# The first layer's memory stage: values for two k tiles ahead of the keys, key weights in 2 KB rows, and the finished values cast ahead of the next group's weights

## The chip, the core and the metric

The kernel runs on one core of one Trainium2 chip. The metric is the device time of one execution in microseconds (us). Three timed runs of the kernel before the change gave 897.07, 897.88 and 898.92 us; the median, 897.88 us, is the number that the change is measured against.

The engines are named as in the profile: PE multiplies matrices (PEld is its weight load, which overlaps), DVE and ACT are the two vector engines that do the casts and subtractions here, POOL issues the small transfers of turned tiles, and SP issues the loads of inputs and weights. All arithmetic on PE is on 32-bit numbers in the format `float32r`.

## The reference, cut to what matters

Two layers; each is one mixer with three head groups (banded chunk attention, gated linear attention, cross-attention into 256 memory tokens), a gate path, an output projection and a layer norm. The change touches only the projection of the memory tokens in the first layer, whose results are the keys and values of the cross-attention:

```python
mkv = mem @ w_mem_kv                    # (256, 2048) @ (2048, 1024)
mk, mv = jnp.split(mkv, 2, axis=-1)     # keys and values, 512 columns each
heads_m = lambda t: t.reshape(t.shape[0], t.shape[1], M_HEADS, M_HEAD_DIM)
y_m = memory_attention(heads_m(m_q), heads_m(mk), heads_m(mv)).reshape(B, S, M_WIDTH)
```

## The kernel before, in words

**Products.** A product in full 32-bit precision is made of three products of split operands: each operand is split into a rounded part `hi` (a cast) and a rest `lo = src - hi`, and `hi*hi + lo*hi + hi*lo` is summed in PSUM. `parts` does one split: the cast on ACT (L128), then the subtraction on DVE (L129). So every weight tile passes from a `raw` tile (the landing place of its DMA) into a `wh` and a `wl` tile, and every activation quarter into the two halves of an `x` tile. `as_products` issues the three matmuls of 128x512 for one k tile (128 of the 2048 inner elements) and one half `t` of the 256 tokens. There are four buffers each of `raw`, `wh` and `wl`.

**The memory stage (`first_memory`).** It comes first in the program. Two accumulators of two banks each are open: `accv` for the values and `acck` for the keys, the only two buffers of their kind. Eight pieces `p` follow each other, each with two k tiles `kk`; `first_pieces` loads and splits one piece: the memory tokens (`memT`, which lands in the space of `res`), the values' weights (a `raw` tile) and the keys' weights (another). The keys' weights lie in DRAM as two column halves of 256 each, and one row of 1024 numbers per partition holds two pieces; a piece's half is 2 k tiles x 256 numbers in a row there.

- For `p` of 0 and 1 the order is written out by hand on every engine: for each k tile the tokens, the values' weights, the keys' weights; PE takes values then keys of k tile 0, then values and keys of k tile 1. In the first k tile the values are cut into two halves of 256 columns, one of them loaded by ACT's queue.
- For `p` from 2 the loads and splits are for whole pieces of 128x1024, and PE takes both k tiles of the values, then both of the keys.
- The keys of piece 6 are kept back (`late`) until after the values of piece 7: the values are then complete, `parts(*mv, accv)` copies them from PSUM into the tiles `mv` (cast on ACT, subtraction on DVE), and PE has the keys of pieces 6 and 7 to go on with meanwhile.

The next group on PE is `as_group(halves(G_BQK), ...)`. It needs an accumulator of the same kind, and so the buffer of `accv`, which is free when both instructions of `mv` have read it. `each(p)` loads and splits a quarter of the layer's input `xT` after pieces 2, 4, 6 and 7 (`resident_quarter`, DMA on L164).

**What sets the order.** PE, SP and POOL work in program order. On ACT and DVE a scheduler that simulates times places the instructions, by priority: what stands under `tc.high_priority(AHEAD)` (the loads and splits of weights and input) goes ahead of what does not (the split into `mv` here). `placed_here` (`tc.keep_in_program_order`) holds an instruction in its place among the others so held. A DMA on SP waits until the buffer it writes is free, and some wait for the landing of an earlier DMA that used the same semaphore; everything behind it on SP waits with it.

Of the kernel before, what the change touches and what calls it, by code (L numbers as in the profile page):

```python
# [36 lines left out]
def hybrid_trunk_kernel(  # L37
# [88 lines left out]
    def parts(hi, lo, src, keep=lambda ins: ins):  # L126

        keep(act.copy(hi, src))  # L128
        keep(dve.tensor_tensor(lo, src, hi.bitcast(F32), op=ALU.subtract))  # L129
# [10 lines left out]
    def piece(src, n, kp=2, home=None):  # L140

        with tc.high_priority(AHEAD):
            raw = wp.tile([P, kp, n], F32, name=nm("raw"), tag="raw")
            if home is None:
                hi, lo = (wp.tile([P, kp, n], F32R, name=nm(w), tag=w) for w in ("wh", "wl"))
            else:
                hi, lo = home
            if isinstance(src, list):
                at = 0
                for part in src:  # L150
                    if len(part.shape) == 2:
                        part = part.rearrange("p (k n) -> p k n", k=kp)
                    sp.dma_start(raw[:, :, at:at + part.shape[2]], part)
                    at += part.shape[2]
            else:
                sp.dma_start(raw.rearrange("p k n -> p (k n)"), src)
            parts(hi, lo, raw)
# [10 lines left out]
    def first_pieces(p, x):  # L168
# [5 lines left out]
        ksrc = w512[0, G_MK, p // 2:8:4, :, j0 * 256:j0 * 256 + 512].rearrange("h p (k n) -> p k h n", k=2)  # L174
        raws, his, los = ([wp.tile([P, 2, 512], dt, name=nm(n), tag=n) for _ in range(2)]
                          for n, dt in (("raw", F32), ("wh", F32R), ("wl", F32R)))

# [8 lines left out]
        def split(i, at):  # L186
            parts(his[i][at], los[i][at], raws[i][at])

        if p < 2:
            with tc.manual_schedule(engines={DVE, mybir.EngineType.Activation}):  # L190
# [6 lines left out]
                for k in range(2):  # L197
                    x_part(slice(j0 + k, j0 + k + 1))
                    for i, at in enumerate(cuts[k]):
                        if i or len(cuts[k]) == 1:  # L200
                            sp.dma_start(raws[0][at], vsrc[at])  # L201
                        split(0, at)
                    sp.dma_start(raws[1][:, k].rearrange("p (h n) -> p h n", h=2), ksrc[:, k])
                    split(1, (slice(None), k))
        else:
            with tc.high_priority(AHEAD):
                x_part(slice(j0, j0 + 2))
                sp.dma_start(raws[0], vsrc)
                split(0, slice(None))
                for h in range(2):  # L210
                    sp.dma_start(raws[1][:, :, h * 256:(h + 1) * 256], ksrc[:, :, h])
                split(1, slice(None))
        return list(zip(his, los))

    def first_memory(mv, each):
# [22 lines left out]
        for p in range(8):  # L238
# [3 lines left out]
            for kk in range(2):  # L242
                values_of(p, v, kk)
                if p < 2:
# [3 lines left out]
            elif p > 1:  # L248
                if p == 7:
                    parts(*mv, accv)  # L250
# [4 lines left out]
            each(p)  # L255
# [10 lines left out]
    def as_group(src, xq, n, kp=2, first=None, need={}):  # L266

        acc = psd.tile([P, 2, 512], F32, name=nm("acc"), tag="acc")
        for pc in range(16 // kp):
# [3 lines left out]
            w = piece(src[pc], n, kp)  # L273
# [563 lines left out]
    for l in range(L):  # L837
# [47 lines left out]
        acc = as_group(halves(G_BQK), xq, 512)  # L885
# [274 lines left out]
```

## Time and profile before

| | |
|---|---|
| timed runs, us | 897.07, 897.88 (median), 898.92 |
| span of the profiled execution, us | 896.4 |
| instructions | 13888 |
| PE busy, us and share of the span | 887.2, 99% |
| DVE busy | 617.4, 69% |
| ACT busy | 482.1, 54% |
| mean granted clock of PE | 0.997 |
| moved by DMA | 216.90 MB, mean 242 GB/s |

The profiled execution has its span on record, from the first to the last instruction, and no timed number of its own; the median of the timed runs is 1.5 us over that span. Times inside the execution are us from the start of the span. In the timeline a row gives start, duration, engine, line, output<-inputs and shape, how many instructions were merged, and in brackets the engine's idle time before and what ended it. The row of a DMA issue (SPq, ACTq) gives the time that issuing took; the view of DMAs gives the time from issue to landing.

### The profile page before, as it was taken

How to read it: one execution, taken by the hardware profiler on the slowest of the kernel's cores; microseconds unless marked ns; L12 is line 12 of the kernel's file. 1: busy time of each engine (PE TensorE's matmuls, PEld its weight loads, DVE VectorE, ACT ScalarE, POOL GpSimd, SP SyncE). 2: the span in 40 equal slices, each digit the busy share in tenths (PEclk: the TensorE clock that was granted, in tenths of full speed). 3: DMA queues.
4: the chain of work that ended last, by engine and by line, in shares of the span. 5: the costliest groups of instructions: out<-in, count | busy, mean ns of one | idle time of the engine just before them, and what ended most of it. 6: DMA issues, size and time to landing. Idle time of an engine off the chain costs nothing.

```text
span 896.4 us, 13888 instructions
## 1 busy us (share of the span) xinstructions
PE 887.2 (99%) x4669; PEld 743.5 (83%) x4669; DVE 617.4 (69%) x905; ACT 482.1 (54%) x698; POOL 231.0 (26%) x431
## 2 busy tenths in 40 slices
PE   9999999999999999999999999999999999999996
PEld 7878988888988888888888888888888888888885
DVE  6756568767467676665595786896664758676866
ACT  6644475555446575543465545754754557565440
POOL 0022103114305353410034230231061444432300
PEclk9999999999999999999999999999999999999998
DMA  9988779867979797975689968696589897979752
GB/s 310 312 241 245 215 245 265 275 197 225 275 253 241 236 274 236 307 241 193 224 267 268 265 195 282 201 287 210 154 234 293 242 260 236 276 222 281 223 179 95
DMA packets 166088, 216.90 MB, mean 242 GB/s; under 512 B 25232, under 2 KB 143376, under 8 KB 166016
## 3 DMA queue, kind: packets, MB, share of 16 engines
q1 hardware_dynamic: 148256, 173.29, 63.7%
q0 software_dynamic: 17472, 42.33, 16.4%
q8 instruction: 37, 0.61, 0.3%
q10 hardware_dynamic: 288, 0.39, 0.1%
q14 instruction: 35, 0.29, 0.1%
HBM read 194.78 MB, written 21.10 MB: 241 GB/s over the span
## 4 chain that ended last, share of the span: by engine, by line
PE 98%; DVE 1%; DMA 0%; ACT 0%; issue 0%; SPq 0%; DVEq 0%
PE acc L102 91%; PE bk L102 6%; DMA raw<-w 0%; ACT wh L128 0%; DVE mv L129 0%; ACT res L823 0%; DVE wl L129 0%; PE bk L665 0%; DVE stats L809 0%; DVE res L808 0%; SPq L201 0%; DVE res L759 0%; SPq L179 0%; DVE mvt L762 0%; PE bk L812 0%
## 5 line engine op out<-in xcount | busy, mean ns | idle before, releaser
L102 PE MATMUL acc<-wh,x 128*128 128x512 f32 (+2 forms) x2516 | 747.8, 381 | 1.3 <-DVE mv L129 0.7
L102 PEld LDWEIGHTS acc<-wh,x 128*128 128x128 f32 x2516 | 460.6, 188 | 88.2 <-PE acc L102 1.1
L129 DVE TENSOR_TENSOR wl<-raw,wh 128x1024 fp32r<-128x1024 f32 (+3 forms) x321 | 368.4, 1152 | 198.9 <-ACT wh L128 187.0
L128 ACT CAST wh<-raw 128x1024 fp32r<-128x1024 f32 (+3 forms) x321 | 318.5, 996 | 344.2 <-PE acc L102 201.7
L102 PE MATMUL acc<-wl,x 128*128 128x512 f32 (+2 forms) x1258 | 475.9, 379 | 0.0
L102 PEld LDWEIGHTS acc<-wl,x 128*128 128x128 f32 x1258 | 236.0, 188 | 45.3 <-DVE wl L129 0.4
L527 POOL DMA_DIRECT2D home<-sc x76 | 42.5, 560 | 426.2 <-DVE sc L525 417.6
L532 POOL DMA_DIRECT2D pT<-home x96 | 52.4, 552 | 30.2 <-DMA home<-sc 12.1
L532 POOL DMA_DIRECT2D qk<-home x64 | 34.9, 553 | 36.5 <-DMA home<-sc 26.2
L532 POOL DMA_DIRECT2D zT<-home x48 | 26.2, 551 | 20.5 <-DMA home<-sc 14.0
L525 DVE STREAM_TRANSPOSE sc<-sc 128x512 f32<-128x512 f32 (+1 forms) x38 | 24.9, 668 | 3.7 <-ACT sc L996 3.0
L532 POOL DMA_DIRECT2D yr<-home x48 | 26.3, 557 | 3.2 <-DMA home<-sc 3.2
L525 DVE STREAM_TRANSPOSE sc<-acc 128x512 f32<-128x512 f32 x28 | 18.3, 691 | 4.3 <-PE acc L102 4.3
L554 ACT ACTIVATE sc<-sc,mx 128x128 f32<-128x128 f32 (+1 forms) x32 | 14.3, 448 | 8.9 <-DVE mx L552 8.8
L547 DVE SCALAR_TENSOR_TENSOR sc<-bk,bias 128x384 f32<-128x384 f32 x16 | 8.6, 539 | 10.7 <-PE bk L102 10.7
L128 ACT CAST x<-sc 128x512 fp32r<-128x512 f32 x20 | 12.2, 617 | 5.2 <-DVE sc L508 3.2
L532 POOL DMA_DIRECT2D xT<-home x24 | 13.2, 552 | 6.9 <-DMA xT<-home 5.2
L129 DVE TENSOR_TENSOR x<-sc,x 128x512 fp32r<-128x512 f32 x20 | 13.5, 685 | 1.4 <-ACT x L128 1.4
L102 PE MATMUL bk<-qk,qk 128*128 128x128 f32 (+1 forms) x64 | 13.1, 326 | 0.0
L698 DVE SCALAR_TENSOR_TENSOR res<-res,acc 128x512 f32<-128x512 f32 x15 | 9.7, 682 | 4.7 <-PE acc L102 4.7
L532 POOL DMA_DIRECT2D yT<-home x16 | 8.8, 555 | 14.8 <-DMA home<-sc 14.8
L129 DVE TENSOR_TENSOR x<-res,x 128x512 fp32r<-128x512 f32 (+2 forms) x13 | 10.0, 790 | 2.0 <-ACT x L128 2.0
(210 smaller groups left out, 524.3 us busy)
## 6 DMA issues: line engine op xcount, KB each, us to landing
raw<-w SPq DMA_DIRECT2D x387, 256.0 KB, 4.6
raw<-w SPq DMA_DIRECT2D x62, 512.0 KB, 5.0
home<-sc POOLq DMA_DIRECT2D x60, 256.0 KB, 4.4
raw<-w SPq DMA_DIRECT2D x32, 388.0 KB, 5.1
raw<-w SPq DMA_DIRECT2D x32, 264.0 KB, 3.5
qk<-home POOLq DMA_DIRECT2D x64, 64.0 KB, 4.7
raw<-w SPq DMA_DIRECT2D x32, 124.0 KB, 4.8
bias<-relw SPq DMA_DIRECT2D x16, 192.0 KB, 4.4
```

The source lines that it names most:

```text
L102: pe.matmul(o, l, r, start=start, stop=stop, skip_group_check=True)
L128: keep(act.copy(hi, src))
L129: keep(dve.tensor_tensor(lo, src, hi.bitcast(F32), op=ALU.subtract))
L525: dve.transpose(blocks.rearrange(order, j=32), src.rearrange("p (g b j) -> p g b j", b=4, j=32))
L527: pool.dma_start(homes[-1], blocks)
L532: pool.dma_start(dst[b * 32:(b + 1) * 32], home[:, b].rearrange("(a i) n -> i a n", a=4))
L547: dve.scalar_tensor_tensor(s, pb[:, :384], SCALE, bias[h], op0=ALU.mult, op1=ALU.add)
L554: act.activation(s[:, own[t]], s[:, own[t]], AF.Exp, bias=mx[:, t:t + 1], accum_out=zs[:, t:t + 1])
L698: dve.scalar_tensor_tensor(r, r, ALPHA, acc, op0=ALU.mult, op1=ALU.add)
```

## The change

- In `first_pieces` for `p` of 0 and 1, tokens and values' weights of both k tiles are loaded and split first, then the keys' weights. PE follows: values of both k tiles, then keys of both.
- The keys' weights of a piece are loaded as they lie: two DMAs, one per column half, each a row of 512 numbers (2 KB) per partition, for every `p`. Before, a DMA read rows of 256 numbers (1 KB): for `p` of 0 and 1 one DMA per k tile with both halves, from piece 2 on one per half. The tile now holds half, k tile, column in that order, and the split reads it through a view that puts the k tile first; `wh` and `wl` are laid out as before. The split of a k tile of the keys now needs both DMAs.
- `each(7)`, the last input quarter, moves ahead of `parts(*mv, accv)`, and the two instructions of `mv` are held in program order. The cast of the first weight piece of `G_BQK` in the first layer is held in program order behind them.

```diff
-    def parts(hi, lo, src, keep=lambda ins: ins):
-        keep(act.copy(hi, src))
+    def parts(hi, lo, src, keep=lambda ins: ins, behind=lambda ins: ins):
+        behind(keep(act.copy(hi, src)))
         keep(dve.tensor_tensor(lo, src, hi.bitcast(F32), op=ALU.subtract))
...
-        ksrc = w512[0, G_MK, p // 2:8:4, :, j0 * 256:j0 * 256 + 512].rearrange("h p (k n) -> p k h n", k=2)
+        ksrc = w512[0, G_MK, p // 2:8:4, :, j0 * 256:j0 * 256 + 512]
...
+        kraw = raws[1].rearrange("p h (k n) -> p k h n", k=2)
...
+        def load_keys():
+            for h in range(2):
+                sp.dma_start(raws[1][:, h], ksrc[h])
+        def split_keys(k):
+            hi, lo = (x[1][:, k].rearrange("p k (h n) -> p k h n", h=2) for x in (his, los))
+            parts(hi, lo, kraw[:, k])
...
-                        split(0, at)
-                    sp.dma_start(raws[1][:, k].rearrange("p (h n) -> p h n", h=2), ksrc[:, k])
-                    split(1, (slice(None), k))
+                        split(at)
+                load_keys()
+                for k in range(2):
+                    split_keys(slice(k, k + 1))
...
             for kk in range(2):
                 values_of(p, v, kk)
-                if p < 2:
+            if p < 2:
+                for kk in range(2):
                     keys_of(p, k, kk)
...
                 if p == 7:
-                    parts(*mv, accv)
+                    each(p)
+                    parts(*mv, accv, placed_here)
...
-            each(p)
+            if p < 7:
+                each(p)
...
-            w = piece(src[pc], n, kp)
+            w = piece(src[pc], n, kp, None, placed_here if pc < kept else lambda ins: ins)
...
-        acc = as_group(halves(G_BQK), xq, 512)
+        acc = as_group(halves(G_BQK), xq, 512, kept=0 if l else 1)
```

How the instructions move is shown at three places. First SP at the start of the program, the queue of loads; `res` is where the tokens land, `raw_113` and `raw_114` are the values' and keys' weights of piece 0, `raw_173` and `raw_174` those of piece 1. Before:

```order
L179 DMA res<-memT 128x256
L201 DMA raw_113<-w 128x256
L203 DMA raw_114<-w 128x2x256
L179 DMA res<-memT 128x256
L201 DMA raw_113<-w 128x512
L203 DMA raw_114<-w 128x2x256
```

Now:

```order
L180 DMA res<-memT 128x256
L210 DMA raw_113<-w 128x256
L180 DMA res<-memT 128x256
L210 DMA raw_113<-w 128x512
L192 DMA raw_114<-w 128x512 x2
L180 DMA res<-memT 128x256
```

The tokens and the values' weights of k tile 1 move up one place each, and both loads of keys stand behind them.

Second PE at the same place, with the scheme of its first products (`acc_110` is `accv`, `acc_111` is `acck`, `x_112` the tokens). Before, after the first tile's values in halves of 256 columns:

```order
L102 MATMUL acc_110<-wl_117,x_112 128x256 x2
L102 MATMUL acc_111<-wh_116,x_112 128x512 x2
L102 MATMUL acc_111<-wl_118,x_112 128x512
L102 MATMUL acc_111<-wh_116,x_112 128x512 x2
L102 MATMUL acc_111<-wl_118,x_112 128x512
L102 MATMUL acc_110<-wh_115,x_112 128x512 x2
```

Now:

```order
L102 MATMUL acc_110<-wl_117,x_112 128x256 x2
L102 MATMUL acc_110<-wh_115,x_112 128x512 x2
L102 MATMUL acc_110<-wl_117,x_112 128x512
L102 MATMUL acc_110<-wh_115,x_112 128x512 x2
L102 MATMUL acc_110<-wl_117,x_112 128x512
L102 MATMUL acc_111<-wh_116,x_112 128x512 x2
```

The second group of six products is now that of the values of k tile 1, not that of the keys of k tile 0; ACT's casts and DVE's subtractions follow the same order.

Third ACT at the end of the stage, where `mv` is cast (`x_481` and `x_455` are the same input quarter under two names, `wh_498` the first weights of `G_BQK`):

```order
 L128 CAST wh_430<-raw_428 128x1024
-L128 CAST x_481<-res 128x4x256
+L128 CAST x_455<-res 128x4x256
+L128 CAST mv_107<-acc_110 128x1024
 L128 CAST wh_498<-raw_497 128x1024
 L128 CAST wh_517<-raw_516 128x1024
-L128 CAST mv_107<-acc_110 128x1024
 L128 CAST wh_544<-raw_543 128x1024
```

The cast of `mv` moves ahead of two weight casts, and on DVE its subtraction moves likewise ahead of those of `wl_499` and `wl_518`. On PE and POOL nothing else moves, and on ACT, DVE and SP nothing after this place.

More of the change, by code (lines that the diff above doesn't have):

```diff
@@ L138, in load_quarter, with piece @@
         return x
-    def piece(src, n, kp=2, home=None):
+    def piece(src, n, kp=2, home=None, behind=lambda ins: ins):
         with tc.high_priority(AHEAD):
@@ L156, in piece @@
                 sp.dma_start(raw.rearrange("p k n -> p (k n)"), src)
-            parts(hi, lo, raw)
+            parts(hi, lo, raw, behind=behind)
         return hi, lo
@@ L184, in x_part, with split @@
                 parts(x[0][:, j], x[1][:, j], xraw[:, j])
-        def split(i, at):
-            parts(his[i][at], los[i][at], raws[i][at])
+        def split(at):
+            parts(his[0][at], los[0][at], raws[0][at])
+        def load_keys():
[4 more added lines that the diff above has]
+            parts(hi, lo, kraw[:, k])
         if p < 2:
@@ L208, in first_pieces @@
                 sp.dma_start(raws[0], vsrc)
[L209 to L212, printed above, removed]
+                split(slice(None))
+                load_keys()
+                split_keys(slice(None))
         return list(zip(his, los))
@@ L264, in as_products, with as_group @@
         mm(o, xh[:, j, ts], wl[:, kk], False, kt == 15)
-    def as_group(src, xq, n, kp=2, first=None, need={}):
+    def as_group(src, xq, n, kp=2, first=None, need={}, kept=0):
         acc = psd.tile([P, 2, 512], F32, name=nm("acc"), tag="acc")
```

## The prediction

> **What bounds the kernel now.** I read the page first, for the busy times:
>
> ```profile
> span 896.4 us, 13888 instructions
> PE 887.2 (99%) x4669; PEld 743.5 (83%) x4669; DVE 617.4 (69%) x905; ACT 482.1 (54%) x698; POOL 231.0 (26%) x431
> ```
>
> PE is idle for 896.4 - 887.2 = 9.2 us in all, and the change adds or removes no product. So it can only gain from idle time of PE, and can only lose by making more. Second, I asked where that idle time is, by stretches (columns: PE, PEld, DVE, ACT, POOL busy with counts, granted clock, DMA share, GB/s) and by what PE waited for:
>
> ```profile
> 0.00:10.00 10.00, 8.29 (x40) 7.01 (x41) 4.32 (x12) 4.73 (x9) 0.20 (x4) 1.00 0.74 217
> 10.00:48.00 38.00, 38.00 (x169) 31.49 (x168) 28.01 (x29) 25.20 (x30) 0.00 (x0) 1.00 0.95 335
> 48.00:51.00 3.00, 2.32 (x10) 1.63 (x10) 3.00 (x4) 2.37 (x3) 0.00 (x0) 1.00 0.63 197
> ...
> PE bk L102 <- DVE eps L836: 1.1, 1, 1.1
> PE bk L812 <- DVE nt L777: 0.9, 1, 0.9
> PE acc L102 <- DVE mv L129: 0.7, 1, 0.7
> PE acc L102 <- ACT wh L128: 0.7, 2, 0.3
> ```
>
> From 10 to 48 us PE has no idle time at all, though the DMA engines are 95% busy. In the part that is edited there are two places with a wait: the first 10 us (two waits of 0.3 for the first weights) and 50 us (0.7 for `mv`). The other waits are at the kernel's beginning and end and are not touched. About 0.2% of the time (1.8 us) is what a measurement of this kernel can tell from no change, and that is more than these two places hold as plain waits.
>
> Third, the timeline at both places. At the start:
>
> ```profile
> 1.66 0.43 SPq L203 DMA_DIRECT2D raw<-w  x1
> 2.12 0.47 SPq L179 DMA_DIRECT2D res<-memT  x1
> 2.63 0.43 SPq L201 DMA_DIRECT2D raw<-w  x1
> 3.11 0.44 SPq L203 DMA_DIRECT2D raw<-w  x1
> ...
> 5.88 0.40 PE L102 MATMUL acc<-wl,x 128*128 128x256 f32 x2
> 5.95 0.62 ACT L128 CAST wh<-raw 128x512 fp32r<-128x512 f32 x1 [1.14 <-DMA raw<-w]
> 6.60 0.69 DVE L129 TENSOR_TENSOR wl<-raw,wh 128x512 fp32r<-128x512 f32 x1 [1.26 <-ACT wh L128]
> 6.62 0.73 PE L102 MATMUL acc<-wh,x 128*128 128x512 f32 x2 [0.34 <-ACT wh L128]
> 7.35 0.50 PE L102 MATMUL acc<-wl,x 128*128 128x512 f32 x1
> 7.68 0.63 PE L102 MATMUL acc<-wh,x 128*128 128x512 f32 x2
> 8.14 0.62 ACT L128 CAST wh<-raw 128x512 fp32r<-128x512 f32 x1 [0.40 <-DMA raw<-w]
> 8.38 0.63 PE L102 MATMUL acc<-wh,x 128*128 128x512 f32 x2
> 8.80 0.69 DVE L129 TENSOR_TENSOR wl<-raw,wh 128x512 fp32r<-128x512 f32 x1 [0.33 <-ACT wh L128]
> 9.06 0.62 PE L102 MATMUL acc<-wh,x 128*128 128x512 f32 x2
> 9.52 0.39 PE L102 MATMUL acc<-wl,x 128*128 128x512 f32 x1
> 9.74 0.62 PE L102 MATMUL acc<-wh,x 128*128 128x512 f32 x2
> ```
>
> In steady running three products begin every 0.68 us (9.06 to 9.74). PE was through with the first values at 6.28 and got the keys' cast at 6.62, because their weights landed just before 5.95. The subtraction for the third product came at 7.29, so that product began at 7.35. Counted back from 7.68 by one step of 0.68, this second group runs as if it had begun at 7.00; unhindered it would have begun 0.23 after 5.88, at 6.11 (two products of 256 columns take as long as one of 512, 0.68 / 3). The start loses 0.89 us here.
>
> At the end of the stage:
>
> ```profile
> 41.09 1.05 ACT L128 CAST x<-res 128x1024 fp32r<-128x1024 f32 x1 [1.76 <-DMA res<-xT]
> 43.46 1.05 ACT L128 CAST wh<-raw 128x1024 fp32r<-128x1024 f32 x1 [1.32 <-DVE x L129]
> 43.52 0.39 PE L102 MATMUL acc<-wl,x 128*128 128x512 f32 x1
> 46.44 1.05 ACT L128 CAST wh<-raw 128x1024 fp32r<-128x1024 f32 x1 [1.93 <-PE acc L102]
> 47.40 1.01 ACT L128 CAST mv<-acc 128x1024 fp32r<-128x1024 f32 x1
> 48.51 0.62 PE L102 MATMUL acc<-wh,x 128*128 128x512 f32 x2
> 48.66 1.22 DVE L129 TENSOR_TENSOR mv<-acc,mv 128x1024 fp32r<-128x1024 f32 x1
> 50.03 0.70 PE L102 MATMUL acc<-wh,x 128*128 128x512 f32 x2 [0.68 <-DVE mv L129]
> 50.80 0.61 PE L102 MATMUL acc<-wh,x 128*128 128x512 f32 x2
> ```
>
> Eight steps of 0.68 before 49.19, PE ends the values: the last product begins at 43.52 and ends at 43.91. From then on ACT could cast `mv`; it does so at 47.40, behind two weight casts, the second of which starts only at 46.44. DVE follows at 48.66 and ends at 49.88, and only then is the accumulator free. PE begins at 50.03 instead of 48.51 + 0.68 = 49.19, which is 0.84, and its first step takes 0.77 instead of 0.68 (50.80 - 50.03), another 0.09.
>
> **The change part by part.** *The cast of `mv` ahead of the weights.* ACT finishes the input quarter at 42.14, so it casts `mv` when the values end, 43.91 to 44.92; DVE (1.22) ends by about 46.4, taking the same 0.25 between the two as in the rows above. That is 2.8 us before PE comes for the accumulator at 49.19. What is late next: the first weights wait behind `mv` on ACT, until 44.92 + 1.05 = 45.97, and on DVE until about 46.4 + 1.2 = 47.6. They are due at 49.19 and, for the third product, 0.46 later, so 3.2 and 2.0 us are left. The second weights start no later than before, at 46.44. The term is the whole of the loss, -0.93; its bounds are -0.93 and 0, where something else would hold PE until 50.
>
> *The order of the first loads.* The values' weights of k tile 1 (256 KB) now take the issue place at 2.12, and the tokens ahead of them the place at 1.66. How long such loads took from issue to landing, in the order of the issues at 1.66, 2.12, 2.63, 3.11 and 4.57:
>
> ```profile
> raw<-w SPq DMA_DIRECT2D x1, 256.0 KB, 4.3
> res<-memT SPq DMA_DIRECT2D x1, 128.0 KB, 4.3
> ...
> raw<-w SPq DMA_DIRECT2D x1, 256.0 KB, 4.5
> ...
> raw<-w SPq DMA_DIRECT2D x1, 256.0 KB, 5.0
> ...
> raw<-w SPq DMA_DIRECT2D x1, 256.0 KB, 5.9
> ```
>
> By the two nearest 256 KB loads (4.3 and 4.5) the weights land at 6.4 to 6.6; I take 6.5, since the bytes issued up to them are exactly those up to the tokens that landed at 2.12 + 4.3 = 6.4. That is 0.55 after the 5.95 at which the keys' weights let PE go on before. The lag from there is the same (a cast of 0.62, a subtraction of 0.69), so the second group comes 0.55 later. The lower bound is a gain of 0.89, if the load is no slower than the kernel's first ones and all stands ready at 6.11:
>
> ```profile
> raw<-w SPq DMA_DIRECT2D x1, 128.0 KB, 3.1
> ```
>
> *The keys in two halves.* Both halves must land before either k tile of the keys can be split. The second is issued in the place at 3.11; with the 5.0 of the load that stood there it lands at 8.1, when the same bytes had landed before (8.14). PE wants these keys as its third group, at 8.38 + 0.55 = 8.93. The cast from 8.14 lets it begin at 8.81, in time; the subtraction ends at 9.49 and its product is due at 8.93 + 0.46 = 9.39. So 0.1 more. In general the start loses 0.55 plus what the landing exceeds 8.05. The upper bound takes 5.9, as for the issue at 4.57: landing at 9.0, a loss of 1.5.
>
> *Rows of 2 KB.* I take no saving from them. The 256 KB in 1 KB rows (4.3, issued at 1.66) and the 256 KB in 2 KB rows (4.5, issued at 2.63) took about the same. From piece 2 on a faster landing would lie under PE's unbroken work between 10 and 48 us and be worth nothing.
>
> The Trainium skill ("DMA: Bandwidth & Descriptors", section Specifications) puts line rate at transfers of 512 B and more, which speaks against any gain, since rows of 1 KB would already have it; the two landings above, 4.3 and 4.5, agree, and no run here isolates it. If rows of 2 KB did speed up the start against that rule, by 0.3 us for the first weights as an estimate, the sum would be 0.3 lower.
>
> *Reading the keys through a view in runs of 256.* Nothing: the `x` tile is written in runs of 256 and its cast takes the 1.05 of the contiguous `wh` beside it. Were it otherwise, ACT and DVE have 12.8 and 10.0 us to spare of the 38 up to 48 us, which cover the six later pieces.
>
> *Moving `each(7)`* changes no place on SP or PE. The loads of pieces 1 and 2 come in the same order and up to half a microsecond sooner or later; PE takes them later too.
>
> The sum: 0.65 lost at the start, 0.93 gained at 50 us, together -0.28 on the span of 896.4. PE is without idle time from there on except where it waits for its own results, so the difference reaches the end. The median stands 1.5 us over the span; carried over, 897.88 - 0.28 = 897.6.
>
> **The rivals.** *The values come in time.* If the weights land by 5.95 or sooner, the start loses nothing or gains up to 0.89, and the time is 897.88 - 0.93 = 896.95 down to 896.06; I put it at 896.5. For it: the tokens are half as large as the keys' weights that stood ahead of them, and the 128 KB quoted last landed in 3.1. Against it: from 3 us on the DMA engines have as much as they can do, and every later load took 4.3 or more.
>
> *The keys come late, and it is slower.* Place: PE's third group, which now waits for two loads, not one. It decides from a landing of 8.43 on, where the start loses 0.93. With 5.9 from issue to landing the loss is 1.5 and the time 897.88 + 1.5 - 0.93 = 898.45. For it: loads issued 1.5 us later took that long, and no other work for PE is in between. Against it: the bytes up to there are those that had landed at 8.14.
>
> *The wait at 50 us stays* because something else holds PE there, the first weights or the input quarter: then only the start counts, 897.88 + 0.65 = 898.5. Against it: the 2 to 3 us of margin worked out above.
>
> **How the numbers follow.** The forecast (897.6, its own range 897.1 to 898.1) has 52%, values in time 25%, keys late 13%, the wait that stays 6%, anything else 4%. The range for 8 in 10 goes from 896.2, most of the second case with the spread of the runs (0.8 to 1.0 around the median), to 898.9, most of the two slow ones. A measured gain above 1.8 us needs the best end of the second case: a fifth of its 25% and a little from elsewhere, 6%. A loss above 1.8 us lies beyond all cases worked out; runs and unknown causes give it 4%. Within 0.2%: 90%.
>
> **What would show it.** Right: no wait of PE for `mv` near 50 us, and the subtraction of `mv` over about 3 us before PE comes for the accumulator; at the start a wait for the values' cast until about 7.2, and a third group that begins about 0.6 after 8.38. If the second group begins at 6.6 or sooner, the values were in time; if the third begins after 9.4, the keys were late. The forecast is wrong if PE shows a new wait between 10 and 48 us, or if a wait after 51 us grows, since nothing was found that the change moves there.

## The result, and the profile after

| | before | after |
|---|---|---|
| median of 22 runs each, us | 897.75 | 899.38 |
| lowest and highest, us | 896.69, 900.28 | 898.34, 901.38 |
| ratio of the times | | 1.0019, interval 1.0013 to 1.0024 |
| profiled execution: span, us | 896.4 | 896.9 |

The change makes the kernel slower by 1.6 us (1.2 to 2.2 by the interval). Forecast were 897.6, a gain of 0.28, and a range up to 898.9: the sign was wrong, and the time lies 0.5 above the range. The ratio itself is just inside the 0.2% that the prediction set as its bound for no change; with 22 runs each, the interval still leaves no change out. The profiled execution of the kernel after took 898.68 as a whole, 0.7 less than its median, so its rows may show somewhat less than the typical loss.

The page of the kernel after, its windows (PE, PEld, DVE, ACT, POOL busy with counts, granted clock, DMA share, GB/s), and PE's waits (total, count, longest):

```profile
span 896.9 us, 13884 instructions
PE 887.6 (99%) x4669; PEld 743.6 (83%) x4669; DVE 616.8 (69%) x905; ACT 481.7 (54%) x698; POOL 231.7 (26%) x431
```

```profile
10.00:48.00 38.00, 38.00 (x168) 31.27 (x167) 28.37 (x32) 25.13 (x31) 0.00 (x0) 1.00 0.91 323
48.00:51.00 3.00, 3.00 (x15) 2.48 (x14) 3.00 (x3) 1.65 (x3) 0.00 (x0) 1.00 0.31 101
```

```profile
PE acc L102 <- ACT wh L128: 1.6, 2, 1.4
PE bk L102 <- DVE eps L848: 1.1, 1, 1.1
PE bk L824 <- DVE nt L789: 0.9, 1, 0.9
PE bk L102 <- ACT nparts L825: 0.3, 1, 0.3
```

The wait for `mv` is gone, from 10 to 48 us PE has no idle time, and the waits at the kernel's beginning and end are as before. One line has grown: the wait for the first weights, 1.6 us in place of 0.7. The start shows where. In its timeline L210 issues the values' weights and L192 the two halves of the keys' weights:

```profile
2.12 0.43 SPq L210 DMA_DIRECT2D raw<-w  x1
2.60 0.91 SPq L192 DMA_DIRECT2D raw<-w  x2
...
5.90 0.40 PE L102 MATMUL acc<-wl,x 128*128 128x256 f32 x2
7.01 0.62 ACT L128 CAST wh<-raw 128x512 fp32r<-128x512 f32 x1 [1.86 <-DMA raw<-w]
7.68 0.73 PE L102 MATMUL acc<-wh,x 128*128 128x512 f32 x2 [1.39 <-ACT wh L128]
8.75 0.63 PE L102 MATMUL acc<-wh,x 128*128 128x512 f32 x2
8.83 1.14 ACT L128 CAST wh<-raw 128x512 fp32r<-128x512 f32 x2 [1.20 <-DMA raw<-w]
9.51 0.73 PE L102 MATMUL acc<-wh,x 128*128 128x512 f32 x2
10.57 0.63 PE L102 MATMUL acc<-wh,x 128*128 128x512 f32 x2
11.27 0.62 PE L102 MATMUL acc<-wh,x 128*128 128x512 f32 x2
11.96 0.62 PE L102 MATMUL acc<-wh,x 128*128 128x512 f32 x2
12.65 0.62 PE L102 MATMUL acc<-wh,x 128*128 128x512 f32 x2
```

A group of six products stands in two such rows. The second group (values of k tile 1) begins at 7.68, 1.06 later than the second group before. The third (keys of k tile 0) begins at 9.51 against 8.38; its step to the next row is 1.06 and not 0.68, because the subtraction for its third product, which needs the same late cast, ends later still. The fourth is at 11.27, and piece 1 begins at 12.65, where it began at 11.11 before. That is 1.54 lost. The DMA view has what was late, in the order of the issues at 2.12, 2.60 and 3.07:

```profile
raw<-w SPq DMA_DIRECT2D x1, 256.0 KB, 4.9
raw<-w SPq DMA_DIRECT2D x1, 256.0 KB, 5.5
raw<-w SPq DMA_DIRECT2D x1, 256.0 KB, 5.7
```

The values landed at 7.0, the keys' second half at 3.07 + 5.7 = 8.8. The other end of the stage:

```profile
45.49 1.02 ACT L128 CAST mv<-acc 128x1024 fp32r<-128x1024 f32 x1 [2.62 <-PE acc L102]
46.54 1.23 DVE L129 TENSOR_TENSOR mv<-acc,mv 128x1024 fp32r<-128x1024 f32 x1 [2.42 <-ACT mv L128]
50.05 0.62 PE L102 MATMUL acc<-wh,x 128*128 128x512 f32 x2
50.73 0.62 PE L102 MATMUL acc<-wh,x 128*128 128x512 f32 x2
```

`mv` is through DVE at 47.77, and PE comes for the accumulator at 50.73, 3 us later, in its steady step of 0.68.

So in this pair of profiles 1.54 is lost at the start and 0.93 gained at 50 us; the difference, 0.6, is about the 0.5 between the two spans. The medians differ by 1.6, though. The experiments had to tell two things: what in the start costs, and where the 0.93 is in the medians.

### The profile page after: what moved, and what is told of

It is laid out like the page before. It is cut to its first block, busy times and chain, and to the rows that moved or that the text cites. A ratio compares the mean times of both kernels' runs of the same rounds, so it can differ in the third digit from the quotient of the medians.

```text
span 896.9 us, 13884 instructions
## 1 busy us (share of the span) xinstructions
PE 887.6 (99%) x4669; PEld 743.6 (83%) x4669; DVE 616.8 (69%) x905; ACT 481.7 (54%) x698; POOL 231.7 (26%) x431
## 4 chain that ended last, share of the span: by engine, by line
PE 98%; DMA 1%; DVE 0%; ACT 0%; SPq 0%; issue 0%
PE acc L102 92%; PE bk L102 6%; DMA raw<-w 1%; ACT res L835 0%; PE bk L677 0%; SPq L180 0%; ACT wh L128 0%; DVE stats L821 0%; DVE res L820 0%; SPq L210 0%; DVE res L771 0%; DVE mvt L774 0%; PE bk L824 0%; ACT nparts L825 0%; DVE rs_u L784 0%
## 5 line engine op out<-in xcount | busy, mean ns | idle before, releaser
L129 DVE TENSOR_TENSOR x<-raw,x 128x1024 fp32r<-128x1024 f32 x5 | 6.1, 1213 | 8.4 <-ACT x L128 8.4
```

## The experiments

Each profile is of one execution. For each the table gives where the second and third group and piece 1 begin (us in the span), how long PE waits for `mv`, and that execution's own time less the begin of its piece 1: all that lies behind the start, and the 1.7 to 2.7 us by which the time exceeds the span. Ratios are against the kernel before, run by turns on the same chip, where its median was 897.84 (beside e1 to e4), 897.91 (e5 to e8), 897.86 (a1 to a4) and 897.98 (t1 to t3). A ratio isn't the quotient of two medians, and the two can differ by some tenths: the median of a2 is 0.54 above that of the kernel before, while its ratio stands for 0.1 us. "Again" marks a kernel that stands in the table twice.

| kernel | 2nd group | 3rd group | piece 1 | `mv` wait | execution less piece 1 | median (runs) | ratio, interval |
|---|---|---|---|---|---|---|---|
| before, first profile | 6.62 | 8.38 | 11.11 | 0.7 | no time of its own | 897.75 (22) | |
| before again, a1 | 6.48 | 7.87 | 10.85 | no | 885.8 | 897.73 (12) | 0.9997, 0.9987-1.0007 |
| before again, a3 | 6.43 | 8.19 | 10.93 | no | 887.9 | profile only | |
| after, first profile | 7.68 | 9.51 | 12.65 | no | 886.0 | 899.38 (22) | 1.0019, 1.0013-1.0024 |
| after again, a4 | 7.99 | 9.81 | 12.94 | no | 887.7 | profile only | |
| e1 `mv` cast first | 6.70 | 8.09 | 10.81 | no | 887.0 | 898.40 (11) | 1.0006, 0.9997-1.0015 |
| the same again, a2 | 7.16 | 8.54 | 11.41 | no | 887.9 | 898.40 (12) | 1.0001, 0.9992-1.0010 |
| e2 start and rows only | 7.31 | 9.59 | 12.76 | 0.6 | 887.0 | 899.77 (9) | 1.0023, 1.0013-1.0032 |
| e3 order only | 7.49 | 9.25 | 11.98 | no | 886.3 | 898.29 (11) | 1.0003, 0.9994-1.0012 |
| e4 late rows only | 7.06 | 8.45 | 11.17 | no | 886.2 | 898.15 (11) | 1.0005, 0.9996-1.0014 |
| e5 first keys per k tile | 7.11 | 8.50 | 11.29 | no | 886.6 | 898.95 (11) | 1.0012, 1.0003-1.0021 |
| e6 e1 and e4 | 6.42 | 8.03 | 10.88 | no | 886.0 | 898.68 (11) | 1.0006, 0.9997-1.0014 |
| e7 first key in halves | 6.83 | 8.26 | 11.01 | no | 887.0 | 897.98 (11) | 1.0001, 0.9992-1.0010 |
| e8 values on ACT's queue | 7.70 | 10.26 | 13.11 | no | 886.5 | 899.28 (11) | 1.0012, 1.0004-1.0021 |
| t1 values in 1 KB rows | 7.24 | 9.59 | 12.71 | no | 885.8 | 898.72 (11) | 1.0012, 1.0003-1.0021 |
| t2 e8 without a pause | 7.17 | 8.94 | 11.68 | no | 886.0 | 897.80 (11) | 1.0000, 0.9991-1.0009 |
| t3 before, no pause | 6.60 | 7.99 | 10.84 | no | 885.9 | 898.12 (11) | 0.9996, 0.9987-1.0005 |

The column "execution less piece 1" is the most useful one. It runs from 885.8 to 887.9 whatever the kernel. Its mean is 886.7 over the eight profiles with the order of the start as before (a1, a3, e1, a2, e4, e6, e7, t3) and 886.5 over the eight with the new one (after, a4, e2, e3, e5, e8, t1, t2). So nearly all that separates the kernels lies ahead of piece 1; behind it single executions differ by 2 us, for reasons that were not followed up, and a difference of a few tenths could not be seen there.

### The three parts of the change

Theory: the start costs some 1.5 and the early cast gains less than it seemed to. Rival: the early cast or the rows cost something further on.

**`e1_values_cast_first`**: the kernel before with the last part of the change alone.

```diff
-                    parts(*mv, accv)
+                    each(p)
+                    parts(*mv, accv, placed_here)
...
-            each(p)
+            if p < 7:
+                each(p)
...
-        acc = as_group(halves(G_BQK), xq, 512)
+        acc = as_group(halves(G_BQK), xq, 512, kept=0 if l else 1)
```

> Only the last part of the change: the finished values are cast ahead of the next weights; the first loads, their order and their rows are as before. Theory (the order of the first loads costs, the early cast gains): PE has no wait for mv at 50 us, 0.93 us of it gone, the time 0.9 below before (ratio 0.9990). Rival (the wait at 50 us is paid again by a later wait of PE, for weights that the cast now delays): no change, and a new wait of PE between 49 and 60 us.

Measured: no wait for `mv` and no new one behind it, 898.40, ratio 1.0006 (0.9997 to 1.0015). A gain of 0.93 would be a ratio of 0.9990, which the interval excludes. The early cast takes a wait away, and no time that could be measured.

**`e2_start_only`**: the changed kernel without the early cast.

```diff
-                    each(p)
-                    parts(*mv, accv, placed_here)
+                    parts(*mv, accv)
...
-            if p < 7:
-                each(p)
+            each(p)
...
-        acc = as_group(halves(G_BQK), xq, 512, kept=0 if l else 1)
+        acc = as_group(halves(G_BQK), xq, 512, kept=0)
```

> The change without its last part: values ahead of the keys in the first two pieces, and the keys in 2 KB rows in all pieces; mv is cast where it was before. Theory: the time is the changed kernel's plus the 0.93 us of the early cast, about 2.5 us above before (ratio 1.0028), and PE's second group of products begins at 7.2 or later instead of 6.6. Rival (the early cast is what costs): the time is that of before.

Measured: 899.77, ratio 1.0023 (1.0013 to 1.0032). The start and the rows carry the loss: the interval covers the 1.0019 of the whole change.

**`e3_order_only`**: the kernel before with values ahead of keys in pieces 0 and 1; the keys are still loaded per k tile in 1 KB rows, one DMA for each.

```diff
                         split(0, at)
+                for k in range(2):
                     sp.dma_start(raws[1][:, k].rearrange("p (h n) -> p h n", h=2), ksrc[:, k])
+                for k in range(2):
                     split(1, (slice(None), k))
...
-                if p < 2:
+            if p < 2:
+                for kk in range(2):
                     keys_of(p, k, kk)
```

> Only the order: in the first two pieces tokens and values of both k tiles ahead of the keys, on every engine; the keys are still loaded in 1 KB rows, one load for each k tile, everywhere; mv is cast as before. Theory (the order costs, since PE's second group now waits for tokens and 256 KB of values): the whole loss of the start, about 2.5 us above before. Rival (the 2 KB rows make the first loads land late): within 0.7 us of before, and the values of k tile 1 land at 6.4 or sooner instead of 7.0.

Measured: 898.29, ratio 1.0003 (0.9994 to 1.0012), 1.48 below e2, which was timed beside it, and the two intervals do not meet. The time is the rival's, but not for its reason: the values landed at 6.79, not by 6.4. K tile 0 of the keys landed at 7.53, k tile 1 at 8.75. The timeline:

```profile
6.82 1.36 ACT L128 CAST wh<-raw 128x512 fp32r<-128x512 f32 x2 [1.07 <-DMA raw<-w]
8.77 0.62 ACT L128 CAST wh<-raw 128x512 fp32r<-128x512 f32 x1 [0.59 <-DMA raw<-w]
9.25 0.63 PE L102 MATMUL acc<-wh,x 128*128 128x512 f32 x2
```

Here two casts follow each other from 6.82, the values' and that of the keys' k tile 0; the third is k tile 1, which landed late and is wanted only as the fourth group. In e2 the cast of the keys stands for both landings:

```profile
8.92 1.14 ACT L128 CAST wh<-raw 128x512 fp32r<-128x512 f32 x2 [1.67 <-DMA raw<-w]
9.59 0.73 PE L102 MATMUL acc<-wh,x 128*128 128x512 f32 x2 [0.36 <-ACT wh L128]
```

Both k tiles are cast one right behind the other, after both halves have landed. By this run the order alone costs about 0.3 (-0.5 to 1.1 by the interval), and loading the keys in halves, so that no k tile can be split until both have landed, costs the rest. The longer rows of the halves are not what makes them late: in e3 the second load of keys, in 1 KB rows, landed at 8.75, in e2, in 2 KB rows, at 8.84.

**`e4_late_rows_only`**: the kernel before with 2 KB rows for the keys from piece 2 on.

```diff
+                kraw = raws[1].rearrange("p h (k n) -> p k h n", k=2)
                 for h in range(2):
-                    sp.dma_start(raws[1][:, :, h * 256:(h + 1) * 256], ksrc[:, :, h])
-                split(1, slice(None))
+                    sp.dma_start(raws[1][:, h], w512[0, G_MK, p // 2 + 4 * h, :, j0 * 256:j0 * 256 + 512])
+                hi, lo = (x[1].rearrange("p k (h n) -> p k h n", h=2) for x in (his, los))
+                parts(hi, lo, kraw)
```

> Only the 2 KB rows of the keys from piece 2 on; the first two pieces and the cast of mv are as before. Theory: no change (ratio 1.0000, within 0.0005), since PE works without a gap from 10 to 48 us before and after. Rival (the longer rows or the split through a view delay a split that PE needs): 0.5 us or more above before with a new wait of PE in that stretch.

Measured: 898.15, ratio 1.0005 (0.9996 to 1.0014): no difference that could be told, and no wait of PE from 10 to 48 us. So e2 less e3 is, but for the few tenths that this interval leaves, the first two pieces' keys.

### Where in the start

**`e5_first_keys_per_tile`**: the changed kernel with the keys of pieces 0 and 1 loaded per k tile, in 1 KB rows again.

```diff
-                load_keys()
+                kboth = w512[0, G_MK, p // 2:8:4, :, j0 * 256:j0 * 256 + 512].rearrange("h p (k n) -> p k h n", k=2)
                 for k in range(2):
-                    split_keys(slice(k, k + 1))
+                    sp.dma_start(raws[1][:, k].rearrange("p (h n) -> p h n", h=2), kboth[:, k])
+                for k in range(2):
+                    parts(his[1][:, k], los[1][:, k], raws[1][:, k])
```

> The changed kernel with one thing undone: in the first two pieces the keys' weights are loaded as before, one load of 256 KB in 1 KB rows for each k tile, so that the first k tile can be split when its own load has landed. Theory (the loss of the start is half the order and half the coupling: no key can be split before both loads landed at 8.7 to 8.9): the third group of products begins at about 9.25 with no wait, piece 1 begins at about 12.0 instead of 12.6, and the time is 0.7 to 1.4 us below the changed kernel, about 898.2. Rival (the order alone costs it all): the time is the changed kernel's, 899.4.

Measured: 898.95, ratio 1.0012 (1.0003 to 1.0021). In its profile the start is nearly as before:

```profile
5.57 0.62 ACT L128 CAST wh<-raw 128x512 fp32r<-128x512 f32 x1 [0.33 <-DMA raw<-w]
7.50 0.62 ACT L128 CAST wh<-raw 128x512 fp32r<-128x512 f32 x1 [1.31 <-DMA raw<-w]
8.50 0.63 PE L102 MATMUL acc<-wh,x 128*128 128x512 f32 x2
```

But this execution took 897.88, 1.07 less than the median, and its values landed at 5.54, earlier than in any other profile with this load in one piece on SP. Up to there after, a4, e2, e3 and e5 issue the same loads in the same order: the values' weights landed at 6.99, 7.30, 6.61, 6.79 and 5.54. The mean is 6.65, close to the 6.5 forecast, in a spread of 1.8. The median of e5 lies between those of e3 and e2, so it doesn't confirm the whole 1.5 for the coupling: uncoupled, the new start costs 0.3 by e3 and 1.1 by e5, and which share of the loss is the order's stays open. Beside e5 the next run, e6, is the fairer measure, since the two differ in nothing but the order of the start.

**`e6_old_start_new_rest`**: e1 and e4 together, which is the whole change except its start; its edits are those two diffs together.

> The changed kernel with the first two pieces undone altogether (order and rows as before); the keys' 2 KB rows from piece 2 on and the early cast of the values stay. Theory: all of the loss is gone, no wait for mv, and the time is that of before or up to 0.9 us below it (897.0 to 897.9), since the wait at 50 us is there in some executions of the kernel before and not in others. Rival (the later parts cost too): 0.5 us or more above before.

Measured: 898.68, ratio 1.0006 (0.9997 to 1.0014). Without the new start no gain or loss is clear of the noise, but the interval goes from a gain of 0.3 to a loss of 1.3, and by the medians this kernel is 0.8 above the one before: the rival's 0.5 isn't excluded. e5 is 0.3 above e6 by medians and 0.5 by ratios, which agrees with the 0.3 of e3 for the order alone.

**`e7_first_key_in_halves`**: e6, where the keys of k tile 0 of piece 0 are cut into two column halves like the values ahead of them, one of them on ACT's queue, so that PE can begin each when it lands.

```diff
+                        act.dma_start(raws[1][:, 0, :256], ksrc[:, 0, 0])
...
+                        sp.dma_start(raws[1][:, 0, 256:], ksrc[:, 0, 1])
+                        for at in cuts[k]:
+                            split(1, at)
...
+            if p == kk == 0:
+                by_halves(acck, w)
+                return
```

> The kernel of the run before with one more edit at the start: the first k tile of the keys is loaded, split and multiplied in two column halves like that of the values, its first half issued on ACT's queue at about 1.15. Theory (PE's second group waits for the landing of one load of 256 KB, which a load of 128 KB issued earlier beats by 0.5 us or more): the second group begins at about 6.1 without a wait and piece 1 at 10.5 or sooner; 0.3 to 0.8 us below the run before. Rival (the landing is set by bytes and by slow loads before 9 us, whatever their size): within 0.2 us of it.

Measured: 897.98, ratio 1.0001 (0.9992 to 1.0010). In the memory stage PE had no wait after its first product, and yet piece 1 began at 11.01, not at 10.5. The second group came at 6.83, because PE ran its first products at half speed until about 6.2. What that is, e8 showed by chance. The median is 0.7 below that of e6, as expected, but the intervals overlap widely and piece 1 began no sooner than the 10.88 of e6, so the theory isn't borne out.

**`e8_values_on_act_queue`**: the changed kernel with the values' weights of k tile 1 issued on ACT's queue at 1.17, which frees a place on SP. If the keys' landing decides, the values' coming early helps little; if the values decide, the time returns.

```diff
+                        act.dma_start(raws[0][:, 1], vsrc[:, 1])
...
-                        if i or len(cuts[k]) == 1:
+                        if (p, k) != (0, 1) and (i or len(cuts[k]) == 1):
```

> The changed kernel with the values' weights of k tile 1 issued on ACT's queue at about 1.15 instead of SP's at 2.12; all else as in the changed kernel, so the keys' two loads move up one place on SP. Theory (both the values and the keys come late, and the keys decide): the second group begins about 1 us sooner, the third still waits for the keys at 8.6 or later, piece 1 begins within 0.3 of 12.6 and the time is the changed kernel's, 899.4. Rival (the late values decide): piece 1 begins a whole 1 us sooner and the time is 1 us below.

Measured: 899.28, ratio 1.0012 (1.0004 to 1.0021), as slow as if the keys had decided. But the reason was another: the values landed at 5.44 and the keys at 6.46 and 7.14, all far earlier than in the kernel after. What held PE stands in its timeline:

```profile
4.97 1.22 PE L102 MATMUL acc<-wh,x 128*128 128x256 f32 x4 [0.56 <-ACT wh L128]
7.70 1.05 PE L102 MATMUL acc<-wh,x 128*128 128x512 f32 x2
8.98 1.05 PE L102 MATMUL acc<-wh,x 128*128 128x512 f32 x2
10.26 0.71 PE L102 MATMUL acc<-wh,x 128*128 128x512 f32 x2
```

and this is the window from 8 to 9 us, columns as above:

```profile
8.00:9.00 1.00, 1.00 (x4) 0.71 (x4) 1.00 (x2) 1.00 (x3) 0.00 (x0) 1.00 1.00 337
```

PE pauses for 0.56 ahead of its first product, because the first loads landed late too (the half of the values on ACT's queue at 4.49, against 4.10 in the kernel after), and then works without idle time in steps of 1.28 instead of 0.68, until 10.26: little more than half speed. The granted clock of 1.00 in the window is no measurement: the trace keeps the granted clock as records with a start and a length, the first record of e8 starts at 10.42, and where there is no record the view prints 1.00.

### Repetitions

**`a1_before_again`** and **`a3_before_look`** are the kernel before, **`a2_cast_first_again`** is e1, **`a4_after_look`** the kernel after. The question was whether anything timed beside the kernel before reads slower by some tenths, as e1, e3, e4 and e6 all came out at 1.0003 to 1.0006, and how often the wait for `mv` is there.

> The kernel before, unchanged, as a second kernel beside itself: how far two groups of executions of one and the same program differ, and a second look at its waits. Theory (the executions of one program spread by some 3 us because the first loads land differently, and the wait for mv at 50 us is there in some of them only): ratio 1.0000 within 0.0008; the look shows another landing of the first loads than the first one did. Rival (whatever is timed beside the kernel before comes out some tenths of a us slower): 0.3 to 0.8 us above before, as four of the variants did.

> The run with the early cast of the values alone, once more, for a tighter interval. Theory (the wait for mv is in about half of the executions of the kernel before, so that its end is worth 0.4 to 0.5 us in the median): 0.2 to 0.9 us below before. Rival (the early cast gives nothing): no change or above, as in the first run.

> A third look at the kernel before: does PE wait for mv at 50 us or not. Theory (it depends on when the second weights of the next group land, since the cast of mv stands behind theirs): a wait only if that cast begins after about 46; none if it begins at 45.5 or sooner.

> A second look at the changed kernel. Theory: no wait for mv; values of k tile 1 land at 6.6 to 7.0, the keys at 8.7 or later, piece 1 begins at 12.5 or later. Rival (the first look was an odd one): the keys by 8.2 and piece 1 by 12.0.

Measured: the kernel before against itself 0.9997 (0.9987 to 1.0007), so such a bias isn't seen. The early cast a second time: 1.0001 (0.9992 to 1.0010), again without a gain. The kernel after a second time has a start like the first (9.81 and 12.94). And neither new profile of the kernel before has a wait for `mv`. PE's waits of a1:

```profile
PE bk L102 <- DVE eps L836: 1.1, 1, 1.1
PE bk L812 <- DVE nt L777: 0.9, 1, 0.9
PE bk L102 <- ACT nparts L813: 0.3, 1, 0.3
```

What decides it is when the second weights of `G_BQK` land, since the cast of `mv` stands behind theirs on ACT. They come in two loads. In the first profile of the kernel before, the row of that cast (46.44) names PE as what ended the idle time, but the second load, issued at 39.65, took

```profile
raw<-w SPq DMA_DIRECT2D x1, 256.0 KB, 6.7
```

and so landed at 46.34, 0.1 ahead of the cast. The timeline of a1, and that of e2:

```profile
44.31 1.05 ACT L128 CAST wh<-raw 128x1024 fp32r<-128x1024 f32 x1 [0.36 <-DMA raw<-w]
45.27 1.01 ACT L128 CAST mv<-acc 128x1024 fp32r<-128x1024 f32 x1
46.54 1.22 DVE L129 TENSOR_TENSOR mv<-acc,mv 128x1024 fp32r<-128x1024 f32 x1
48.92 0.61 PE L102 MATMUL acc<-wh,x 128*128 128x512 f32 x2
```

```profile
48.05 1.05 ACT L128 CAST wh<-raw 128x1024 fp32r<-128x1024 f32 x1 [2.55 <-DMA raw<-w]
49.01 1.00 ACT L128 CAST mv<-acc 128x1024 fp32r<-128x1024 f32 x1
50.27 1.22 DVE L129 TENSOR_TENSOR mv<-acc,mv 128x1024 fp32r<-128x1024 f32 x1
```

In a1 that cast starts at 44.31 and `mv` is free 1.8 before PE wants it at 49.60; in e2 it starts at 48.05 and PE waits 0.6. In the kernels that cast `mv` late it started at 46.44 in the first profile (a wait), at 44.31, 44.91, 45.35, 44.12 and 45.35 in a1, a3, e3, e4 and t3 (none), each time 0.1 after the second load had landed. The wait is in 2 of 7 profiles. A wait of 0.93 in 2 of 7 executions would be worth some 0.3 in the mean, as an estimate; the interval of e1 reaches just that far, and that of a2 farther.

### What the start of PE depends on

**`t1_values_in_1kb_rows`**: the changed kernel with the values' weights of k tile 1 in two loads of 128 KB with 1 KB rows, in the same place.

```diff
-                        if i or len(cuts[k]) == 1:
+                        if (p, k) == (0, 1):
+                            for h in range(2):
+                                half = (slice(None), 1, slice(h * 256, (h + 1) * 256))
+                                sp.dma_start(raws[0][half], vsrc[half])
+                        elif i or len(cuts[k]) == 1:
```

> The changed kernel with the values' weights of k tile 1 in two loads of 128 KB, each a column half in 1 KB rows; one split, as before, when both have landed; so one load more on SP. Theory (the length of the rows does not matter; 256 KB that are issued at 2.1 and stand behind three loads of 128 KB land late because the DMA engines move less from 5 to 7 us): the values land at 6.6 or later and the time is the changed kernel's or a little above, 899.4 to 899.9. Rival (the 2 KB rows make the load late): the values land by 6.2, and the time is 0.4 us or more below the changed kernel.

Measured: 898.72, ratio 1.0012 (1.0003 to 1.0021). The values landed at 5.45 and 6.49, the keys at 8.15 and 8.84:

```profile
6.57 0.62 ACT L128 CAST wh<-raw 128x512 fp32r<-128x512 f32 x1 [1.39 <-DMA raw<-w]
8.92 1.14 ACT L128 CAST wh<-raw 128x512 fp32r<-128x512 f32 x2 [1.73 <-DMA raw<-w]
9.59 0.73 PE L102 MATMUL acc<-wh,x 128*128 128x512 f32 x2 [0.42 <-ACT wh L128]
```

The values come 0.5 earlier than in the first profile after, but the spread of that load (5.54 to 7.30) holds this landing too, so the length of the rows isn't settled. It settles something else: with the values at 6.5 the third group still begins at 9.59. In the four profiles of this order whose keys are coupled (after, a4, e2, t1) it begins at 9.51, 9.81, 9.59 and 9.59, whether the values land at 6.49 or at 7.30, and each time 0.67 or 0.68 after the cast of the keys has begun; in the two that are not (e3, e5), at 9.25 and 8.50, straight behind the second group.

**`t2_act_queue_no_pause`**: e8 with nine zero products instead of seven ahead of the first product, so that PE doesn't pause. **`t3_before_no_pause`**: the same two more in the kernel before.

```diff
-    for _ in range(7):
+    for _ in range(9):
```

> The run with the values of k tile 1 on ACT's queue, and two more products of zeros at the start (9 instead of 7, 0.43 us each by the rows of the first timeline), so that PE is busy until the first tokens are split at about 4.9. Theory (the pause of 0.56 kept PE at half speed until 10.3 us, and that alone ate the earlier landings): PE is at full speed by 8 us at the latest, the keys land at 7.2, piece 1 begins at 10.5 to 11.3 instead of 13.1, and the time is 1.5 us or more below that run: 896.8 to 897.8. Rival (the clock has nothing to do with the pause): half speed to 8 us or later again, and 899 or more.

> The control: the kernel before with 9 products of zeros instead of 7, nothing else. Theory: in the kernel before the pause is 0.3 us and PE reaches full speed between 4.7 and 7.1 anyway, behind which it waits for keys; the two more products end at about 5.1, so the first product begins about 0.5 later, and the time is 0 to 0.5 us above before. Rival (the pause costs the kernel before too): 0.3 us or more below before.

Measured, t2: 897.80, ratio 1.0000 (0.9991 to 1.0009), 1.5 below e8 by the medians. PE is at full speed from about 5.6:

```profile
5.30 0.87 PE L102 MATMUL acc<-wh,x 128*128 128x256 f32 x4
7.17 0.73 PE L102 MATMUL acc<-wh,x 128*128 128x512 f32 x2
```

So it was most likely the pause that made e8 slow: without it half speed ends 4.8 sooner. It isn't beyond doubt, since the intervals of e8 and t2 still share 1.0004 to 1.0009 and each half speed was seen in one execution. Piece 1 begins at 11.68, later than expected; the first product came only at 5.30, behind the extra zero products and first loads that landed later still (4.65 and 4.84). With values and keys early and no pause the new order is as fast as the kernel before, within 0.8 us either way, not faster. t3: 898.12, ratio 0.9996 (0.9987 to 1.0005), no difference. No version was measurably faster than the kernel before.

## Why the prediction was wrong, step by step

**The keys in two halves** (0.1 forecast): the step that failed most. The mechanism was right. The formula, 0.55 plus what the landing exceeds 8.05, gives 0.55 + 0.75 = 1.3 for the 8.8 measured, and the rows show 1.54; most of the rest is that PE's step behind the late third product is 0.34 instead of 0.23 (10.23 to 10.57). The landing was mis-sized: 5.0 from issue was taken over from the load that had stood in that place, with the argument that the bytes up to there were the same. The second half landed at 8.75, 9.06 and 8.84 in after, a4 and e2, 5.7 and more after its issue. The bound of 5.9 taken from the next load was the better estimate. "The keys come late" named the place (the third group) and the sign of the result, with 13%; its price of 898.45 was too low mainly because it still counted the 0.93. Its threshold, a landing at 8.43, was passed in all four coupled profiles of this order, and its sign, a third group after 9.4, was there in all four.

**The order of the first loads** (0.55 forecast, values at 6.5): the mean of five profiles, 6.65, is near; the first of the kernel after, 6.99, and the second, 7.30, are not, and in the first the second group alone is 1.06 late. By ratios this part alone costs 0.3 (e3) or, with the rest of the change, 1.1 (e5; 0.5 above e6). The 0.89 that the kernel before was said to lose here was also that one execution's: in a1, e1, a2, e4 and t3 PE was at half speed longer, came to the second group at 6.48 to 7.16 and did not wait for the keys' cast. Together with the halves the start costs, by the begin of piece 1, 12.8 (mean of after, a4 and e2) less 11.0 (mean of the first profile before and of the eight others with the old order), 1.8, where 0.65 was forecast.

**The cast of `mv` ahead** (-0.93): done as described, with the forecast margin of about 3 us and no new wait behind it. But its worth was read from one execution whose weights landed late. The wait stood in 1 of 3 profiles of the kernel before and in 2 of 7 in all; e1, timed twice, shows no gain. So the term is 0 to 0.3, not 0.93. The lower bound of the term, 0, was given, but with the wrong condition: not that something else holds PE at 50 us, but that there is mostly no wait.

**The sum**: 1.8 less 0 to 0.3 is close to the 1.6 measured; 0.65 - 0.93 was the forecast. Two terms were off, each by 0.6 to 1.2 us and in the same direction. The 1.8 rests on three profiles, so that the sum comes out this well is partly luck.

**Right**: no idle time of PE from 10 to 48 us; the rows of 2 KB from piece 2 on are worth nothing that could be measured (e4); a cost of reading the keys through a view and of moving `each(7)` isn't seen, though e6 leaves room for some tenths; "values in time" did not come true; "the wait at 50 us stays" did not either. The 0.3 that a gain from 2 KB rows in the first weights was put at has no row behind it, and none was seen: the second load of keys in this order landed at 8.75 and 8.49 in 1 KB rows (e3, e5) and at 8.75, 9.06 and 8.84 in 2 KB rows (after, a4, e2), and t1 lies within the spread of one load. The Trainium skill ("DMA: Bandwidth & Descriptors", section Specifications), by which rows of 1 KB already have line rate, is not contradicted by these.

**Open**: why the same 1280 KB, up to the keys of piece 0, have landed at 8.5 to 9.1 in the new order and at 7.7 to 8.3 in the old one, and how the loss divides between order (0.3 to 1.1), coupling and, by e6, perhaps some tenths behind the start.

## What to carry to other kernels

A wait seen in one profiled execution can be priced when it hangs on compute; if it hangs on when a load lands, as that for `mv` did, take a second profile before pricing its removal. At the start of a kernel, where nothing is queued for PE, a split that needs two loads starts when the later one lands: cut the first loads by what is consumed first, not by how they lie in DRAM, and price a landing by the worst neighbour rather than the nearest. Subtracting the start's last event from an execution's time shows, over several profiles, whether two kernels differ in the start or behind it.

## What the hardware showed that was not expected

**PE at half speed at the start, where the view of the clock shows nothing.** In e8 PE works in steps of 1.28 up to 10.26 and of 0.68 afterwards. In the other profiles, too, the first products begin 0.21 apart until some moment, and those of 256 columns 0.12 apart behind it. That moment is where the trace's first record of the granted clock (1.0) starts: in each of the 17 profiles the steps are long ahead of it and short behind it, but for the restart from a wait. It was 3.9 in the first profile before, 4.3 in the first after, 5.0 in a4, 5.4 and 5.2 in a1 and a3, 5.9 in e1, 7.1 in a2 and 10.4 in e8, with its pause of 0.56; in t2, without the pause, it was 5.6. Ahead of the first record nothing is written down, and the views count that stretch as 1.00. So at a kernel's start the step between products, or the start of the first record, shows the speed, not the number in the view. A pause of 0.39 (e2, 6.8) did not put the moment off beyond what kernels without a pause show (a2, 7.1).

The Trainium skill ("TensorE: Matmul & The Clock Gate", section "Part 1: The HAM clock gate (the "warmup" mystery)") says that the clock is halved until a window of about 3.4 us has been busy, and that clock records of a trace are not always reliable. The first agrees with this case: the record of full speed is 884.05, 887.47 or 890.88 us long in the 17 profiles, in steps of 3.41, and 10.42 lies between one and two such windows behind the pause of e8. The window need not be busy throughout, since in the first profile before full speed came 2.9 us after PE's first product at 1.05; how much of a pause it bears was not isolated. The records themselves fit the steps here.

**Loads of the first microseconds.** From 5 to 7 us (window rows as above, of after, a1 and e8):

```profile
5.00:7.00 2.00, 1.30 (x11) 1.09 (x9) 0.70 (x3) 0.15 (x1) 0.00 (x0) 1.00 0.81 209
```

```profile
5.00:7.00 2.00, 2.00 (x15) 1.84 (x15) 1.21 (x4) 1.03 (x2) 0.00 (x0) 1.00 0.99 313
```

```profile
5.00:7.00 2.00, 2.00 (x9) 2.00 (x10) 1.50 (x5) 1.33 (x3) 0.00 (x0) 1.00 1.06 396
```

With all the early 256 KB loads on SP's queue, the new order moved 209 to 257 GB/s there (after, a4, e2, e3, e5, t1) and the old one 268 to 313 (before, a1, a3). With one of them on ACT's queue it was 396 (e8) and 394 (t2); with half of one there, in the old order, 305 (e7), no more than without. The loads are of the same bytes; the cause was not isolated.

**The spread of one program.** The kernel before took 896.6 to 900.8 on one chip, and behind its start a1 and a3 differ by 2 us. Several terms of a forecast of this size lie below that.
